# Eight experts on one core: the first weight load goes behind GpSimd's memsets, and ScalarE takes casts from VectorE

## The chip, the core and the metric

The kernel runs on one core of a Trainium2 chip. A core has TensorE (matmul), VectorE, ScalarE, GpSimd and SyncE (SP), each with its own instruction stream, and 16 DMA engines that move data between the chip's memory (DRAM) and the core's on-chip memories SBUF and PSUM. In the profile TensorE is PE with its weight loads as PEld, VectorE is DVE, ScalarE is ACT, GpSimd is POOL. DMAs are issued here by SP (loads and stores without a change of type) and by GpSimd (the weights, which are cast from fp32 to fp16 on the way, and some of the rest). The metric is the device time of one execution in microseconds (us), as the median of several runs; lower is better.

## The reference

Eight experts, each with 256 rows of x (512 wide), a hidden layer of 2048 with bias and ReLU, and an output layer of 512 with bias. All inputs are fp32, and so is the output.

```python
n_experts, capacity, hidden, expert_hidden = 8, 256, 512, 2048
h = np.matmul(x, w1) + b1[:, np.newaxis, :]
h = np.maximum(h, 0)
return (np.matmul(h, w2) + b2[:, np.newaxis, :]).astype(np.float32)
```

Each expert has a w1 of 512 x 2048 and a w2 of 2048 x 512, 4 MB each in fp32, 2 MB (2048 KB) as fp16 in SBUF. All weights together are 64 MB to be read once.

## The kernel before

**Stages.** The kernel goes through the experts with a lag: step s does the first layer of expert s (four matmuls over 512 inputs for each of 16 blocks j of 128 hidden units, line 289, into the four PSUM tiles `ph`) and, from step 3 on, the second layer of expert s - 3 (b2 by a matmul with ones at line 304, then 32 matmuls at line 319 into `po`). ScalarE evicts each `ph` with bias and ReLU to `hT` (line 107) and moves finished `po` to the output tiles (line 119); for the last two experts VectorE evicts half.

**Loads and queues.** GpSimd's queue carries, in this order: w1 of expert 0 and b2 (lines 349 to 353, ahead of everything else on GpSimd), w1 of experts 1 and 2, and then in turn w1 of expert s, w2 of expert s - 3, and at step 4 x of the last four experts. There are three buffers each for w1 and w2, so a load from the fourth on waits until the matmuls have finished with its buffer (`ph_full` and `po_full`). SP's queue carries x of expert 0, x of expert 1, b1, and x of experts 2 and 3 (line 348), and at the end two of the stores.

**The head.** `first_loads` and `first_turns` are ordered by a planner, which places semaphores by the data that each instruction needs. GpSimd sets four small tiles (lines 357 to 360); VectorE turns a block of them (361) and ScalarE copies from it an identity matrix (364). VectorE casts x of experts 0 and 1 to fp16 (366); TensorE turns them with the identity (373) and VectorE copies the result to `xT` (374). VectorE also turns b1 (376). Then comes the section (`tile_critical`, lines 382 to 389), whose semaphores are written out by hand. All engines but GpSimd enter it once all that was issued ahead of it is done, loads included; GpSimd goes in without that wait, issues w1 of experts 1 and 2, and waits for the same things at `wait_critical_data_deps`. In the section ScalarE casts x of experts 2 and 3 (194), and VectorE turns them (223). SP waits for each weight load and raises the counts `w1_in` and `w2_in`, for which TensorE waits.

Of the kernel before, what the change touches and what calls it, by code (L numbers as in the profile page):

```python
# [10 lines left out]
def kernel(  # L11
# [9 lines left out]
    nc = tc.nc  # L21
# [3 lines left out]
    E, T, H = x.shape  # L25
# [3 lines left out]
    nKC = H // P  # L29
# [4 lines left out]
    NW = 3  # L34
# [5 lines left out]
    GROUP_OF = {f + i: (f, n) for f, n in GROUPS.items() for i in range(n)}  # L40
# [11 lines left out]
    w1_sb = w1_f[:, 0 : NW * nKC * M].rearrange("p (n kc m) -> p n kc m", n=NW, kc=nKC)  # L52
    w2_sb = sb("w2sb", [P, NW, nJ, H])
    hT = sb("hTsb", [P, NH, nJ, T])
    xT = sb("xTsb", [P, NX, nKC, T])
    x16 = {f: sb(f"x16_{f}", [P, n * nTB, H]) for f, n in FIRST.items()}
    grouped = {f: sb(f"outg{f}", [P, n * nTB, H], fp32) for f, n in GROUPS.items()}
    pair = [sb(f"pair{i}", [P, nTB, H], fp32) for i in range(2)]
    b2_sb = sb("b2sb", [1, E * H])
# [10 lines left out]
    def sem(name):  # L70
        return nc.alloc_semaphore(name)

    s_x = sem("s_x")
    s_w1 = {e: sem(f"s_w1_{e}") for e in range(1, E)}
    s_w2 = {(e, h): sem(f"s_w2_{e}_{h}") for e in range(E) for h in range(2 if e in CUT else 1)}
    s_out = {e: sem(f"s_out{e}") for e in (0, 4, E - 2)}
    memsets = sem("memsets")
    cast = sem("cast")
    xT_full = sem("xT_full")
    w1_in = sem("w1_in")  # L80
# [5 lines left out]
    po_free_d = sem("po_free_d")  # L86
# [36 lines left out]
    def scalar_from(e):  # L123

        return 0 if e in GROUP_OF else nTB // 2
# [4 lines left out]
    x32 = {e: pair[e] for e in range(2)}  # L130
    x32[2] = grouped[0][:, 0 : FIRST[2] * nTB, :]

    def w1_of(e):
        return w1[e].rearrange("(p kc) m -> p kc m", kc=nKC)

    def x_of(first):
        n = FIRST[first]
        return x[first : first + n].rearrange("e (p r) h -> (e p) r h", r=n * nTB)
# [1 line left out]
    def run_sync():  # L140
        s = nc.sync
        for step in range(E + LAG):
            if step < E:
                if step in s_w1:
                    s.wait_ge(s_w1[step], 16)
                s.sem_inc(w1_in, 1)  # L146
            if step >= LAG:
                e = step - LAG
                for h in range(2):
                    if (e, h) in s_w2:  # L150
                        s.wait_ge(s_w2[e, h], 16)
                    s.sem_inc(w2_in, nQ // 2)  # L152
                    if e == E - 1 and h == 0:
                        s.wait_ge(po_free_a, E)
                        s.wait_ge(po_free_d, E)
                        s.dma_start(out=out_of(E - 2, 1), in_=pair[0]).then_inc(s_out[E - 2], 16)

    def run_gpsimd():
        g = nc.gpsimd

        def load_w1(e):
            if e >= NW:
                g.wait_ge(ph_full, nJ * (e - NW + 1))
            g.dma_start(out=w1_sb[:, e % NW], in_=w1_of(e)).then_inc(s_w1[e], 16)  # L164

        def load_w2(e):
            if e >= NW:
                g.wait_ge(po_full, ENDS * (e - NW + 1))
            src = w2[e].rearrange("(p j) h -> p j h", j=nJ)
            cuts = (0, CUT[e], nJ) if e in CUT else (0, nJ)  # L170
            for h, (lo, hi) in enumerate(zip(cuts, cuts[1:])):
                g.dma_start(  # L172
                    out=w2_sb[:, e % NW, lo:hi], in_=src[:, lo:hi]).then_inc(s_w2[e, h], 16)

        for step in range(1, E + LAG):
            if step < E:
                if step == 4:
                    g.dma_start(out=x16[step], in_=x_of(step)).then_inc(s_x, 16)
                load_w1(step)
            if step == NW - 1:  # L180
                tc.wait_critical_data_deps()
            if step >= LAG:
                load_w2(step - LAG)
        g.wait_ge(s_w2[E - 1, 0], 16)
        for first in sorted(GROUPS, reverse=True):
            done = 1 + first + GROUPS[first]
            g.wait_ge(po_free_a, done)
            g.dma_start(out=out_of(first, GROUPS[first]), in_=grouped[first]).then_inc(  # L188
                s_out[first], 16)
    def run_scalar():  # L190
        a = nc.scalar
        a.sem_inc(ph_free, NPH)
        a.sem_inc(po_free_a, 1)  # L193
        a.copy(out=x16[2], in_=x32[2]).then_inc(cast, 1)  # L194
        for step in range(E + LAG):
            if step < E:
                for j in range(nJ):
                    a.wait_ge(ph_full, nJ * step + j + 1)
                    relu(step, j).then_inc(ph_free, 1)
            if step >= LAG:  # L200
                e = step - LAG
                a.wait_ge(po_full, ENDS * (e + 1))
                for k in range(result(e)[3]):
                    ins = evict(e, scalar_from(e), nTB, k, a.copy)
                ins.then_inc(po_free_a, 1)

    def run_vector():
        v = nc.vector
        v.sem_inc(po_free_d, 1 + len(GROUP_OF))
        v.sem_inc(xT_full, 2)  # L210
        def turn(e):
            first, n, at = X_OF[e]
            R, wide = n * nTB, P // n
            if at == 0:
                v.wait_ge(*((cast, 1) if first == 2 else (s_x, 16)))
            if e >= NX:
                v.wait_ge(ph_full, nJ * (e - NX + 1))
            to = xT[:, e % NX].rearrange("p kc (r i) -> p kc r i", r=R)
            for half in range(wide // B):
                p0 = at * wide + half * B  # L220
                for b in range(nB):
                    src = x16[first][p0 : p0 + B, :, b * (H // nB) : (b + 1) * (H // nB)]
                    ins = v.transpose(  # L223
                        out=to[b * B : (b + 1) * B, :, :, half * B : (half + 1) * B],
                        in_=src.rearrange("p r (i kc) -> p kc r i", kc=nKC))
            ins.then_inc(xT_full, 1)

        turn(2)
        turn(3)
        for e in range(E):  # L230
            if e + NX < E:
                turn(e + NX)
            if scalar_from(e):
                v.wait_ge(po_full, ENDS * (e + 1) - 1)
                for k in range(result(e)[3]):
                    ins = evict(e, 0, scalar_from(e), k, v.tensor_copy)
                ins.then_inc(po_free_d, 1)

    def run_tensor():
        t = nc.tensor  # L240
        mult, mod, least = (getattr(mybir.AluOpType, n) for n in ("mult", "python_mod", "min"))
        xT_f = xT.rearrange("p n kc t -> p (n kc t)")
        w2_f = w2_sb.rearrange("p n j h -> p (n j h)")
# [25 lines left out]
        with t.Fori(0, E + LAG) as s:  # L269
            with t.If(s < E):  # L270
# [8 lines left out]
                with t.Fori(0, nJ // NPH):  # L279
                    w1_j = val(w1_at, (NW - 1) * nKC * M + nJ - NPH)  # L280
                    for i in range(NPH):
                        if i % 2 == 0:
                            t.wait_ge(ph_free, val(due, E * nJ, 1))
                        for kc in range(nKC):
                            if kc % 2 == 0:
                                ahead(w1_cols(w1_j, i, kc), w1_cols(w1_j, i, kc + 1), weights=True)
                            if i % 2 == 1 and kc == nKC - 1:
                                t.reg_add(due, due, 2)
                            ins = t.matmul(  # L289
                                out=ph[i][:, 0:T],  # L290
# [9 lines left out]
            with t.If(s >= LAG):  # L300
                o = val(o_at, nTB * 512)
                b_e = val(b_at, (E - 1) * H)
                for tb in range(nTB):
                    t.matmul(  # L304
                        out=po_f[:, bass.ds(o + tb * 512, H)],
# [6 lines left out]
                with t.Fori(0, nQ):  # L312
# [4 lines left out]
                    for tb in range(nTB):  # L317
                        for j in range(QJ):
                            ins = t.matmul(  # L319
                                out=po_f[:, bass.ds(o + tb * 512, H)],  # L320
# [20 lines left out]
    def first_loads():  # L341
        for to, rows in (
            (x32[0], x_of(0)),
            (x32[1], x_of(1)),
            (b1_rows, b1.rearrange("e (b i) -> (e b) i", b=nB)),
            (x32[2], x_of(2)),
        ):
            tc.keep_in_program_order(nc.sync.dma_start(out=to, in_=rows))  # L348
        for to, rows in (
            (w1_sb[:, 0], w1_of(0)),  # L350
            (b2_sb, b2.rearrange("e h -> (e h)").rearrange("(o f) -> o f", o=1)),
        ):
            tc.keep_in_program_order(nc.gpsimd.dma_start(out=to, in_=rows))

    def first_turns():
        g, v, a, t = nc.gpsimd, nc.vector, nc.scalar, nc.tensor
        g.memset(steps, 0.0)
        g.memset(ident, 0.0)
        g.memset(ones1, 1.0)
        g.memset(steps.rearrange("p n c -> p (n c)")[:, :: B + 1], 1.0)  # L360
        v.transpose(out=steps_turned, in_=steps)  # L361
        for b in range(nB):
            part = slice(b * B, (b + 1) * B)
            a.copy(out=ident[part, part], in_=steps_turned[part, :, 0])  # L364
        for e in range(2):
            v.tensor_copy(out=x16[e], in_=x32[e])  # L366
        for e in range(2):
            pt = ph[2 + e].bitcast(fp16)
            to = pt.rearrange("p (kc r i) -> p kc r i", kc=nKC, r=nTB)
            for r in range(nTB):  # L370
                rows = x16[e][:, r, :].rearrange("p (i kc) -> p kc i", kc=nKC)
                for kc in range(nKC):
                    t.transpose(out=to[:, kc, r, :], in_=rows[:, kc, :], identity=ident)  # L373
            v.tensor_copy(out=xT[:, e], in_=pt.rearrange("p (kc t) -> p kc t", kc=nKC))  # L374
        for b in range(nB):
            v.transpose(  # L376
                out=b1T[b * B : (b + 1) * B, nB - 1 - b : nB - 1 - b + nJ * B],
                in_=b1_rows.rearrange("r (i j) -> r j i", j=nJ))
# [49 lines left out]
```

## Time and profile before

| what | value |
|---|---|
| time, median of 3 runs | 180.91 us (180.85 to 181.17) |
| the profiled execution's own time | 180.94 us |
| its span, first to last instruction | 178.8 us |
| TensorE busy | 131.9 us (74%) |
| ScalarE busy | 82.3 us (46%) |
| VectorE busy | 40.5 us (23%) |
| GpSimd's DMA queue, share of 16 engines | 95.2% |
| moved by DMA, mean rate | 40.98 MB, 229 GB/s |

Times in the trace are counted from the start of the span. A row of the order of time reads: start, duration, engine, line, operation, output<-input, number of instructions, and in brackets the engine's idle time before it and what ended it. POOLq, SPq and so on are the instruction streams where they issue DMAs. In rows by stretch each engine has its busy time and number of instructions; then come TensorE's granted clock, the mean busy share of the DMA engines and the rate. DMA rows count fp16 bytes for the weights, as they are written, while twice as many are read.

### The profile page before, as it was taken

To read this page: it belongs to the slowest core of one execution; us is meant where nothing else is said; L and a number is where in the kernel's file an instruction comes from. 1 tells how busy PE (TensorE), PEld (TensorE's weight loads), DVE (VectorE), ACT (ScalarE), POOL (GpSimd) and SP (SyncE) were. 2 spreads that over 40 slices of the span, in tenths; PEclk is the share of its full clock that TensorE was granted. 3 is DMA by queue.
4 is the path that set the end of the run, shared out by engine and by line. 5 is a ranking of instruction groups with operands and counts; after the bars stand their busy time and mean duration, and the time that the engine had idled before them with its cause. 6 is when DMAs were issued, how large, how long until landed. Compare 5 with 4: busy or idle time off the path is not lost.

```text
span 178.8 us, 2881 instructions
## 1 busy us (share of the span) xinstructions
PE 131.9 (74%) x800; PEld 87.4 (49%) x800; DVE 40.5 (23%) x43; ACT 82.3 (46%) x156; POOL 13.8 (8%) x30
## 2 busy tenths in 40 slices
PE   0002299696969995899959995799599997998940
PEld 0002178575858742785348643674178543443410
DVE  0274399500000299992000000000000000001010
ACT  2002448585867804883098506970488303131010
POOL 7200000302020101001010001000200002001000
PEclk9999999999999999699987999999969999999995
DMA  5999989999999998998998999999899899999995
GB/s 206 278 255 273 236 176 235 235 202 209 236 220 191 235 224 187 235 231 180 235 235 191 220 235 213 198 235 224 187 235 231 180 235 205 205 235 202 323 456 249
DMA packets 3825, 40.98 MB, mean 229 GB/s; under 512 B 448, under 2 KB 464, under 8 KB 1136
## 3 DMA queue, kind: packets, MB, share of 16 engines
q0 software_dynamic: 3056, 37.76, 95.2%
q1 hardware_dynamic: 768, 3.21, 4.6%
q14 instruction: 1, 0.01, 0.0%
HBM read 71.39 MB, written 4.19 MB: 423 GB/s over the span
## 4 chain that ended last, share of the span: by engine, by line
DMA 62%; PE 18%; ACT 6%; DVE 6%; issue 2%; SPq 1%; ACTq 0%; DVEq 0%
DMA w1sb<-in_w_dram 43%; DMA outg<-in_x_dram 10%; PE ph L289 10%; DMA w2sb<-in_w_dram 9%; PE po L319 8%; DVE xTsb L223 6%; ACT hTsb L107 5%; ACT x L194 1%; SPq L348 1%; PE po L304 0%; ACT pair L119 0%; ACTq L423 0%; SPq L146 0%; SPq L152 0%; ACTq L193 0%
## 5 line engine op out<-in xcount | busy, mean ns | idle before, releaser
L289 PE MATMUL ph<-xTsb,w1sb 128*128 x512 | 69.0, 295 | 20.6 <-SPq L146 9.2
L289 PEld LDWEIGHTS ph<-xTsb,w1sb 128*128 x512 | 59.4, 148 | 31.4 <-issue 28.1
L107 ACT ACTIVATE hTsb<-ph,b1T 128x256 f16<-128x256 f32 x128 | 56.9, 475 | 15.4 <-PE ph L289 15.1
L319 PE MATMUL po<-w2sb,hTsb 128*128 x256 | 56.8, 379 | 1.7 <-SPq L152 1.6
L319 PEld LDWEIGHTS po<-w2sb,hTsb 128*128 x256 | 25.0, 98 | 32.3 <-issue 4.8
L119 ACT COPY outg<-po 32x1024 f32<-32x1024 f32 (+1 forms) x20 | 20.1, 1007 | 43.3 <-PE po L319 43.2
L223 DVE STREAM_TRANSPOSE xTsb<-x 32x512 f16<-32x512 f16 (+1 forms) x32 | 31.0, 969 | 31.1 <-DMA x<-in_x_dram 27.7
L119 DVE COPY pair<-po 128x512 f32<-128x512 f32 x2 | 1.4, 692 | 88.0 <-PE po L319 88.0
L373 PE MATMUL ph<-ident,x 128*128 128x128 f16 x16 | 1.9, 308 | 16.8 <-ACT ident L364 16.8
L172 POOL DMA_DIRECT2D w2sb<-in_w_dram x10 | 5.3, 534 | 70.4 <-PE po L319 70.4
L373 PEld LDWEIGHTS <-x 128*128 128x128 f16 x16 | 1.6, 142 | 16.7 <-issue 16.7
L164 POOL DMA_DIRECT2D w1sb<-in_w_dram x7 | 4.2, 599 | 64.4 <-PE ph L289 64.2
L119 ACT COPY pair<-po 128x512 f32<-128x512 f32 x2 | 1.2, 586 | 13.4 <-PE po L319 13.4
L364 ACT COPY ident<-hTsb 32x32 f16<-32x32 f16 x4 | 1.0, 240 | 13.6 <-DVE hTsb L361 13.6
L304 PE MATMUL po<-b2sb,ones 1*128 x16 | 4.8, 378 | 0.9 <-issue 0.8
L376 DVE STREAM_TRANSPOSE b1T<-b1rows 32x512 f32<-32x512 f32 x4 | 4.1, 1022 | 4.1 <-DMA b1rows<-in_b_dram 4.1
L194 ACT CAST x<-outg 128x2048 f16<-128x2048 f32 x1 | 1.9, 1899 | 3.7 <-DMA outg<-in_x_dram 3.7
L304 PEld LDWEIGHTS po<-b2sb,ones 1*128 1x128 f16 x16 | 1.5, 91 | 3.6 <-issue 3.3
L366 DVE CAST x<-pair 128x1024 f16<-128x1024 f32 x2 | 1.4, 694 | 4.7 <-DMA pair<-in_x_dram 4.7
L188 POOL DMA_DIRECT2D out_dram<-outg x2 | 1.1, 538 | 16.1 <-DMA w2sb<-in_w_dram 16.1
L374 DVE COPY xTsb<-ph 128x1024 f16<-128x1024 f16 x2 | 1.4, 692 | 2.4 <-PE ph L373 2.4
L364 ACT ACT_TABLE_LOAD x1 | 1.3, 1283 | 0.7 <-PEq L412 0.7
(12 smaller groups left out, 5.0 us busy)
## 6 DMA issues: line engine op xcount, KB each, us to landing
w1sb<-in_w_dram POOLq DMA_DIRECT2D x8, 2048.0 KB, 30.4
w2sb<-in_w_dram POOLq DMA_DIRECT2D x6, 2048.0 KB, 43.6
w2sb<-in_w_dram POOLq DMA_DIRECT2D x2, 1024.0 KB, 27.8
out_dram<-outg POOLq DMA_DIRECT2D x1, 2048.0 KB, 11.5
w2sb<-in_w_dram POOLq DMA_DIRECT2D x1, 1280.0 KB, 16.8
pair<-in_x_dram SPq DMA_DIRECT2D x2, 512.0 KB, 3.8
outg<-in_x_dram SPq DMA_DIRECT2D x1, 1024.0 KB, 17.8
x<-in_x_dram POOLq DMA_DIRECT2D x1, 1024.0 KB, 27.9
```

Of the source, the lines that this page charges most:

```text
L107: return nc.scalar.activation(out=to, in_=columns, func=relu_of, bias=b1T[:, at : at + 1], scale=1.0)
L119: return copy(out=t.rearrange("p (tb s) h -> p tb s h", s=split)[at : at + rows, lo:hi, k, :], in_=po[k * rows : (k + 1) * rows, e % 2, lo ...
L164: g.dma_start(out=w1_sb[:, e % NW], in_=w1_of(e)).then_inc(s_w1[e], 16)
L172: g.dma_start(out=w2_sb[:, e % NW, lo:hi], in_=src[:, lo:hi]).then_inc(s_w2[e, h], 16)
L194: a.copy(out=x16[2], in_=x32[2]).then_inc(cast, 1)
L223: ins = v.transpose(out=to[b * B : (b + 1) * B, :, :, half * B : (half + 1) * B], in_=src.rearrange("p r (i kc) -> p kc r i", kc=nKC))
L289: ins = t.matmul(out=ph[i][:, 0:T], lhsT=w1_cols(w1_j, i, kc), rhs=x_cols[kc], start=(kc == 0), stop=(kc == nKC - 1),)
L304: t.matmul(out=po_f[:, bass.ds(o + tb * 512, H)], lhsT=ones1, rhs=b2_sb[0:1, bass.ds(b_e, H)], start=True, stop=False, skip_group_check=True,)
L319: ins = t.matmul(out=po_f[:, bass.ds(o + tb * 512, H)], lhsT=hT_f[:, bass.ds(h_e + (j * T + tb * P), P)], rhs=w2_f[:, bass.ds(w_e + j * H, ...
L364: a.copy(out=ident[part, part], in_=steps_turned[part, :, 0])
L373: t.transpose(out=to[:, kc, r, :], in_=rows[:, kc, :], identity=ident)
L376: v.transpose(out=b1T[b * B : (b + 1) * B, nB - 1 - b : nB - 1 - b + nJ * B], in_=b1_rows.rearrange("r (i j) -> r j i", j=nJ))
```

## The change

There are four edits, all at the head of the program.

1. The loads of w1 of expert 0 and of b2 leave `first_loads` and become the first two issues of GpSimd in the section. So they stand behind the four memsets on GpSimd. They get semaphores of their own: SP now waits for the load of expert 0 as for the others, and TensorE waits for b2 as its first act in the section. These two loads are no longer among what the engines wait for when they enter the section.
2. ScalarE instead of VectorE casts x of experts 0 and 1.
3. Of the two copies of turned x from PSUM to `xT`, that of expert 1 goes to ScalarE.
4. Two increments of semaphores at the start of the section go from VectorE to ScalarE.

As the planner orders it, VectorE's head is then: the turn of the small block, two of the four b1 turns, the copy of expert 0's turned x, the other two b1 turns. Before, it was: the two casts, four b1 turns, the turn of the small block, the two copies. ScalarE's head is: four identity copies, the two casts, the copy of expert 1's turned x.

```diff
-    s_w1 = {e: sem(f"s_w1_{e}") for e in range(1, E)}
+    s_w1 = [sem(f"s_w1_{e}") for e in range(E)]
+    s_b2 = sem("s_b2")
...
     def run_sync():
-                if step in s_w1:
-                    s.wait_ge(s_w1[step], 16)
+                s.wait_ge(s_w1[step], 16)
                 s.sem_inc(w1_in, 1)
...
     def run_gpsimd():
+        load_w1(0)
+        g.dma_start(
+            out=b2_sb, in_=b2.rearrange("e h -> (e h)").rearrange("(o f) -> o f", o=1)
+        ).then_inc(s_b2, 16)
         for step in range(1, E + LAG):
...
     def run_scalar():
         a.sem_inc(po_free_a, 1)
+        a.sem_inc(po_free_d, 1 + len(GROUP_OF))
+        a.sem_inc(xT_full, 2)
         a.copy(out=x16[2], in_=x32[2]).then_inc(cast, 1)
...
     def run_vector():
-        v.sem_inc(po_free_d, 1 + len(GROUP_OF))
-        v.sem_inc(xT_full, 2)
...
     def run_tensor():
         t = nc.tensor
+        t.wait_ge(s_b2, 16)
...
     def first_loads():
-        for to, rows in (
-            (w1_sb[:, 0], w1_of(0)),
-            (b2_sb, b2.rearrange("e h -> (e h)").rearrange("(o f) -> o f", o=1)),
-        ):
-            tc.keep_in_program_order(nc.gpsimd.dma_start(out=to, in_=rows))
...
     def first_turns():
         for e in range(2):
-            v.tensor_copy(out=x16[e], in_=x32[e])
+            a.copy(out=x16[e], in_=x32[e])
...
-            v.tensor_copy(out=xT[:, e], in_=pt.rearrange("p (kc t) -> p kc t", kc=nKC))
+            copy = (v.tensor_copy, a.copy)[e]
+            copy(out=xT[:, e], in_=pt.rearrange("p (kc t) -> p kc t", kc=nKC))
```

More of the change, by code (lines that the diff above doesn't have):

```diff
@@ L73 @@
     s_x = sem("s_x")
-    s_w1 = {e: sem(f"s_w1_{e}") for e in range(1, E)}
+    s_w1 = [sem(f"s_w1_{e}") for e in range(E)]
+    s_b2 = sem("s_b2")
     s_w2 = {(e, h): sem(f"s_w2_{e}_{h}") for e in range(E) for h in range(2 if e in CUT else 1)}
     s_out = {e: sem(f"s_out{e}") for e in (0, 4, E - 2)}
-    memsets = sem("memsets")
     cast = sem("cast")
@@ L131 @@
     x32[2] = grouped[0][:, 0 : FIRST[2] * nTB, :]
-    def w1_of(e):
-        return w1[e].rearrange("(p kc) m -> p kc m", kc=nKC)
     def x_of(first):
@@ L163, in load_w1 @@
                 g.wait_ge(ph_full, nJ * (e - NW + 1))
-            g.dma_start(out=w1_sb[:, e % NW], in_=w1_of(e)).then_inc(s_w1[e], 16)
+            g.dma_start(out=w1_sb[:, e % NW], in_=w1[e].rearrange("(p kc) m -> p kc m", kc=nKC)).then_inc(s_w1[e], 16)
         def load_w2(e):
```

## The prediction

> **What bounds the kernel now.** I read the page first, then busy time by stretches, then the chain of waits.
>
> ```profile
> span 178.8 us, 2881 instructions
> PE 131.9 (74%) x800; PEld 87.4 (49%) x800; DVE 40.5 (23%) x43; ACT 82.3 (46%) x156; POOL 13.8 (8%) x30
> DMA  5999989999999998998998999999899899999995
> q0 software_dynamic: 3056, 37.76, 95.2%
> q1 hardware_dynamic: 768, 3.21, 4.6%
> ```
>
> No compute engine is near full: TensorE is busy for 74% of the span, all others for less than half. The row of the DMA engines stands at 8 or 9 tenths in 38 of its 40 slices, and GpSimd's queue (q0, all the weights) holds 95.2% of the engines' time. The stretches say it without the rounding of slices; the last two columns are the DMA share and GB/s, and a packet is counted where it begins, so that a share can pass 1.
>
> ```profile
> core 0: us, PE busy (x) PEld busy (x) DVE busy (x) ACT busy (x) POOL busy (x), PEclk, DMA share, GB/s
> 0.00:2.50 2.50, 0.00 (x0) 0.00 (x0) 0.00 (x0) 1.28 (x1) 1.45 (x7) 1.00 0.21 49
> 2.50:4.75 2.25, 0.00 (x0) 0.00 (x0) 0.59 (x1) 0.00 (x0) 2.09 (x5) 1.00 1.02 410
> 20.00:40.00 20.00, 15.87 (x112) 13.58 (x112) 11.24 (x16) 13.99 (x28) 1.59 (x3) 1.00 0.98 210
> 40.00:80.00 40.00, 33.19 (x232) 25.55 (x232) 18.30 (x15) 26.01 (x54) 3.18 (x6) 0.96 1.02 216
> 80.00:120.00 40.00, 33.66 (x210) 22.43 (x208) 1.48 (x2) 23.43 (x44) 1.59 (x3) 0.96 1.02 216
> 120.00:164.00 44.00, 40.08 (x202) 21.14 (x202) 0.69 (x1) 16.01 (x26) 2.12 (x4) 0.96 1.02 216
> 172.00:176.00 4.00, 0.00 (x0) 0.00 (x0) 0.00 (x0) 0.51 (x1) 0.00 (x0) 0.78 0.95 406
> 2.50:177.50 175.00, 131.91 (x800) 87.42 (x800) 40.51 (x43) 81.02 (x155) 12.39 (x24) 0.96 1.02 233
> ```
>
> From 2.5 to 177.5 us, 175 of the 178.8 us, the 16 DMA engines are full (share 1.02), in each long stretch as in the sum. The weights go at a steady 216 GB/s, so one weight load of 2048 KB (2.1 MB as it is written) occupies them for 2.1 / 0.216 = 9.7 us. The chain of waits shows the same from the other side:
>
> ```profile
> 2.12 17.83 DMA outg<-in_x_dram
> 42.44 28.68 DMA w1sb<-in_w_dram
> 81.71 47.53 DMA w1sb<-in_w_dram
> 147.57 16.84 DMA w2sb<-in_w_dram
> 164.60 3.62 PE po L319 x16
> 168.26 3.64 PE po L319 x16
> 171.92 0.59 ACT pair L119
> ```
>
> A w1 load that needs 9.7 us lands 28.68 and 47.53 us after its issue: the rest is standing in the queue behind earlier loads. The end is set by the last w2 load (its first part lands at 147.57 + 16.84 = 164.41), then 7.3 us of matmul, an eviction and the stores. So the span is the start of the DMA stream, plus its total work, plus idle time of its engines, plus this tail. An edit counts only as far as it changes one of these four.
>
> **The change part by part.** *The first w1 load behind the memsets.* The head of GpSimd's program and of SP's:
>
> ```profile
> 0.74 0.86 SPq L348 DMA_DIRECT2D pair<-in_x_dram  x2
> 1.25 0.67 POOL L353 DMA_DIRECT2D w1sb<-in_w_dram  x1 [0.80 <-POOLq L412]
> 2.41 0.98 POOL L357 MEMSET hTsb<- 128x1024 f16 x1
> 3.98 1.53 POOL L164 DMA_DIRECT2D w1sb<-in_w_dram  x2 [0.16 <-issue]
> ```
>
> From the first of four memsets to the first issue in the section are 3.98 - 2.41 = 1.57 us, entry to the section included. In the changed kernel the memsets start where the w1 load of expert 0 does now (1.25), and that load is issued at 1.25 + 1.57 = 2.82. The b2 load and the w1 loads of experts 1 and 2 follow in the same order, so the queue's order is unchanged, and every later issue of GpSimd waits for matmuls as before. What does the delay of 1.57 us do to the engines?
>
> ```profile
> 4.50:4.75 0.25, 0.00 (x0) 0.00 (x0) 0.25 (x1) 0.00 (x0) 0.25 (x1) 1.00 0.96 393
> 4.75:5.00 0.25, 0.00 (x0) 0.00 (x0) 0.10 (x1) 0.00 (x0) 0.25 (x2) 1.00 4.68 1000
> 5.00:6.00 1.00, 0.00 (x0) 0.00 (x0) 0.62 (x1) 0.00 (x0) 0.51 (x1) 1.00 0.09 20
> ```
>
> And SP's loads of the head, by size and time from issue to landing (us):
>
> ```profile
> pair<-in_x_dram SPq DMA_DIRECT2D x2, 512.0 KB, 3.8
> outg<-in_x_dram SPq DMA_DIRECT2D x1, 1024.0 KB, 17.8
> b1rows<-in_b_dram SPq DMA_DIRECT2D x1, 64.0 KB, 8.5
> ```
>
> The jump to 1000 GB/s at 4.75 to 5.00 is the beginning of the long weight packets: share 4.68 of 0.25 us is 1.17 us of work laid on every engine at once, which runs through the nearly empty row behind it. So the w1 load's data begins some 3.6 us after its issue (4.85 - 1.25). Until then the x loads of SP's queue alone fill the engines, at 410 GB/s. That queue holds 2 x 512 + 1024 + 64 KB, 2.16 MB; the two halves for experts 0 and 1 (1.05 MB) are through at about 4.9, and the rest, b1 and x of experts 2 and 3 (1.11 MB), would last 1.11 / 0.41 = 2.7 us more, to 7.6. These are the loads that now take 8.5 and 17.8 us to land, because they share the engines with w1. If the w1 load's data begins 3.6 us after the new issue, at 6.4, the engines still have 1.2 us of x to carry: no idle time, and what was done first is only done second. Cost: nothing. The cover is the x of experts 2 and 3; without it the cost would be 6.4 - 4.9 = 1.5 us. The unknown is the 3.6 us. Its lower end doesn't matter (any start before 7.6 costs nothing). For its upper end I take the slowest neighbour:
>
> ```profile
> L164 POOL DMA_DIRECT2D w1sb<-in_w_dram x7: 530/530/999, 4.0 to 81.7; - x7
> ```
>
> and what ran beside that one:
>
> ```profile
> 4.16 0.69 DVE L366 CAST x<-pair 128x1024 f16<-128x1024 f32 x1 [4.16 <-DMA pair<-in_x_dram]
> ```
>
> An issue at line 164 takes 530 ns, one of the seven 999, the one at the section's start, beside VectorE's cast. Even with 0.47 us for that and as much as a whole transpose of VectorE (1.25 us, quoted below) in the way, the data would begin at 8.1, and the idle time would be 0.5 us. I take 6.4, since it is the same instruction with the same queue before it.
>
> The Trainium skill, page "SBUF — State Buffer", section "SBUF: two separate sides", says that a VectorE copy or cast in its two-port mode locks GpSimd out of writing the descriptors of its DMAs, so that such a DMA starts late. The 999 ns beside the cast agree with it, though one case shows no cause. By that page the change, which takes both casts from VectorE, would let the w1 load's data begin sooner after its issue than 3.6 us, and the rival below of idle engines would fall away; the sum would stay at nothing, because an earlier start finds the engines full of x.
>
> *Casts, eviction and VectorE's order.* VectorE's list becomes the turn of the identity's steps, two b1 turns, one xT copy, two b1 turns; ScalarE gets both casts and the other xT copy. What the pieces take and when they end now:
>
> ```profile
> 10.19 4.13 DVE L376 STREAM_TRANSPOSE b1T<-b1rows 32x512 f32<-32x512 f32 x4 [4.11 <-DMA b1rows<-in_b_dram]
> 14.35 1.25 DVE L361 STREAM_TRANSPOSE hTsb<-hTsb 128x1024 f16<-128x1024 f16 x1
> 15.62 1.00 ACT L364 COPY ident<-hTsb 32x32 f16<-32x32 f16 x4 [13.60 <-DVE hTsb L361]
> 16.77 1.87 PE L373 MATMUL ph<-ident,x 128*128 128x128 f16 x16 [16.77 <-ACT ident L364]
> 22.09 10.15 PE L289 MATMUL ph<-xTsb,w1sb 128*128 x64 [3.46 <-issue]
> ```
>
> ```profile
> L194 ACT CAST x<-outg 128x2048 f16<-128x2048 f32 x1 | 1.9, 1899 | 3.7 <-DMA outg<-in_x_dram 3.7
> ```
>
> Today the steps' turn stands behind the b1 turns, which wait for b1 until 10.19. In the changed kernel the memsets end near 2.7, the turn (1.25) near 3.9, the identity's copies (1.00) near 4.9, ScalarE's two casts (half of 1.9 us each, by the cast of twice the width) near 6.8, the PE turns (1.87) near 8.7, the copies out near 10. VectorE's four b1 turns (4.13), once b1 has landed near 7, end near 12. All engines then wait at the section's entry for x of experts 2 and 3; it shares the engines with w1 from 6.4 on and lands at 13 to 17. The first w1 matmul can't start before w1 itself: 7.6 us of stream plus 9.7 is 17.3, plus b2 behind it and the waits, about 18.5. So this part has 5 us of cover, and brings the first matmuls from 22.09 to about 18.5. That is not on the path: the w1 load of expert 3 would be issued about 4 us earlier, into a queue that still holds the loads of experts 1 and 2 (to 7.6 + 3 x 9.7 = 36.7). What is late next is the stream itself. Cost and gain: nothing.
>
> *New waits.* SP waits for the first w1 load before it raises its count, and TensorE waits for b2 once. Behind them stand stage 0's matmuls and nothing else; b2 is 8 KB next in the queue. With 4 us in hand, nothing.
>
> **Sum.** 0 for the w1 load, 0 for the casts and the order, 0 for the waits; I add 0.1 us as an estimate for fewer switches between the two queues, since the share stands at 1.02 where both overlap a little. The profiled execution took 180.94 us (span 178.8 and 2.1 around it), 0.03 over the median of 180.91. Forecast 181.0.
>
> **Rivals.**
> *The engines run dry at the head (slower).* The x of experts 2 and 3 isn't ready behind the first two, and the engines stand idle from 4.9 until the w1 load's data begins. For it: today b1 and that x land 8.5 and 17.8 us after their issue, and no row shows them alone. Against: both were issued by about 2.1, and the engines never had a gap in which to show it. Place: 4.9 to 7.6 us; it decides from the moment at which the w1 data begins with nothing else queued. Full price 6.4 - 4.9 = 1.5, which gives 182.4; with only a late start after the x, up to 0.5, 181.4.
> *The chain is right as it is drawn (faster).* The chain runs through x of experts 2 and 3, its cast, its turns and the first two stages of matmuls; if the issues made earlier by this really pulled the stream, all would move by 22.09 - 18.5, 3.6 us, to 177.3. For it: the order of the chain. Against: no stretch has spare engines to take the earlier issues. A smaller gain would need the same spare time.
> *The compute becomes late (slower).* If ScalarE's longer list or the wait for b2 kept stage 0 back so long that the w1 load of expert 3 came after 36.7, the queue would run dry. With a start at 18.5 and 10.15 us for the stage it is issued near 29; 8 us would have to be lost. Each us beyond that costs one: with 10 us lost, 183.
>
> **How the numbers follow.** Forecast 0.64, with its own range 180.6 to 181.3; engines dry at the head 0.20; the chain right or any spare time found 0.12; late compute 0.04. About 0.2% (0.36 us) is what a measurement of this kernel can tell from no change. The two slower rivals make 0.24, the faster one 0.12, the forecast 0.64. The range runs from 180.5 up to the full price of dry engines, 182.4; what it leaves out is most of the faster rival and the late compute.
>
> **What would show it.** Right: the share of 2.5 to 177.5 us stays at 1.02, with no empty stretch between 5 and 8 us that no long packets cover; the GpSimd row of the first w1 load stands near 2.8, the x of experts 2 and 3 lands well before 17.8 us after its issue, the first w1 matmul is near 18.5, and the last w2 load's landing stays within 0.3 us of 164.41. Wrong: a stretch near 5 to 6.5 us at a share far below 1 with no packets begun before it, or the last w2 landing moved by more than 0.3 us.

## The result and the profile after

The changed kernel takes 181.64 us (median of 13 runs, 180.85 to 181.95) against 180.96 us of the kernel before (13 runs, 180.85 to 181.25): a ratio of 1.0031, 95% interval 1.0019 to 1.0043. It is slower by 0.6 (the ratio) to 0.7 us (the medians). The forecast was 181.0, no change. 181.64 lies in the range that was given, 180.5 to 182.4, but above the forecast's own range of 180.6 to 181.3, which had most of the chance. The profiled execution took 181.65 us.

The page after, the parts that were shown of before:

```profile
span 179.9 us, 2874 instructions
PE 132.7 (74%) x800; PEld 87.7 (49%) x800; DVE 38.5 (21%) x40; ACT 85.5 (48%) x159; POOL 13.4 (7%) x30
q0 software_dynamic: 3056, 37.76, 94.7%
q1 hardware_dynamic: 768, 3.21, 4.9%
```

The same bytes on the same queues. The weights' queue holds 94.7% of a longer span, and SP's queue (q1) holds 4.9% instead of 4.6% for the same 3.21 MB. The stretches after:

```profile
core 0: us, PE busy (x) PEld busy (x) DVE busy (x) ACT busy (x) POOL busy (x), PEclk, DMA share, GB/s
2.50:4.75 2.25, 0.00 (x0) 0.00 (x0) 0.92 (x1) 1.24 (x5) 2.12 (x4) 1.00 1.02 400
4.75:5.75 1.00, 0.18 (x2) 0.18 (x3) 0.00 (x0) 0.77 (x1) 0.00 (x0) 1.00 1.02 193
1.50:25.00 23.50, 6.22 (x36) 4.78 (x37) 9.83 (x12) 8.37 (x13) 2.90 (x8) 1.00 1.00 249
20.00:40.00 20.00, 16.99 (x120) 14.55 (x121) 11.25 (x16) 14.02 (x30) 1.59 (x3) 1.00 1.02 218
40.00:80.00 40.00, 31.34 (x215) 23.86 (x214) 17.22 (x14) 24.06 (x50) 3.18 (x6) 0.91 1.02 217
80.00:120.00 40.00, 33.78 (x210) 22.53 (x209) 2.56 (x3) 23.38 (x43) 1.59 (x3) 0.96 1.02 217
```

From 20 us on the rates are those of before (216). In the first 25 us, before and after:

```profile
1.50:25.00 23.50, 4.78 (x30) 3.94 (x31) 10.79 (x13) 4.42 (x9) 3.85 (x8) 1.00 1.03 260
```

260 GB/s before, 249 after. All x loads of SP's queue are through by 25 us in both, so what is missing, 11 GB/s x 23.5 us = 0.26 MB, is weights, and at 0.216 MB per us that is 1.2 us of stream. (This is coarse: a packet is counted where it begins, and 0.26 MB is just one packet of 16 KB on each of the 16 engines.) Most of it goes missing right behind the x of experts 0 and 1: SP's loads move at 400 GB/s up to 4.75 us, and at 193 GB/s in the us behind it. A row of 193 GB/s at a share of 1.02 could also be weights, which go at 216, but no packet of the weights' queue q0 begins in it:

```profile
q1 hardware_dynamic: 75, 0.19, 102.0%
```

So SP's own packets take longer there. The trace's single packets say how much: the first seven pieces of 8 KB of the x of experts 2 and 3 take 1.0 to 1.3 us each, and most of the later ones 0.31 to 0.32, as from the first one on in the kernel before. The second weight load, by the mean end of its last 16 packets, is 0.85 us late, and stays so to the end. That is about the sum of what the first 25 us lose: 0.2 us more of idle time per engine, and 0.7 us more of SP packets that take longer than is usual for their size. A load has landed with its last packet, and that comes 0.9 to 1.1 us late. The whole lag is there again at the end, in the chain of waits:

```profile
148.81 16.69 DMA w2sb<-in_w_dram
165.69 3.62 PE po L320 x16
169.36 3.64 PE po L320 x16
173.02 0.59 ACT pair L119
```

The first part of the last w2 load lands at 148.81 + 16.69 = 165.50, 1.09 us later than before (164.41); behind it the tail is as before. The head of the two issuing programs:

```profile
0.74 0.95 POOL L353 MEMSET hTsb<- 128x1024 f16 x1 [0.29 <-POOLq L409]
0.74 0.86 SPq L349 DMA_DIRECT2D pair<-in_x_dram  x2
2.12 0.42 SPq L349 DMA_DIRECT2D outg<-in_x_dram  x1
2.36 0.67 POOL L160 DMA_DIRECT2D w1sb<-in_w_dram  x1 [0.22 <-issue]
```

The w1 load of expert 0 is issued at 2.36 (2.82 was forecast: the memsets start at 0.74, half a us sooner than the load did), 1.1 us later than before. When does its data begin? The rows of a quarter us rise when its packets of 16 KB join:

```profile
5.50:5.75 0.25, 0.18 (x2) 0.18 (x3) 0.00 (x0) 0.01 (x1) 0.00 (x0) 1.00 0.92 254
5.75:6.00 0.25, 0.25 (x5) 0.25 (x4) 0.00 (x0) 0.11 (x1) 0.00 (x0) 1.00 0.99 270
6.00:6.25 0.25, 0.25 (x5) 0.25 (x4) 0.00 (x0) 0.25 (x1) 0.00 (x0) 1.00 1.69 393
6.25:6.50 0.25, 0.25 (x4) 0.09 (x1) 0.13 (x1) 0.25 (x1) 0.00 (x0) 1.00 2.08 492
```

It joins at about 6: 13 of its first 16 packets begin from 5.75 to 6.5, the other three after 7, where before 15 of them began at 4.75 to 5.00. The first w1 matmul starts at 20.87 (22.09 before), and that is worth nothing: the loads end later all the same.

### The profile page after: what moved, and what is told of

Same layout as the page of the kernel before. It is cut to its first block, busy times and chain, and to the rows that moved or that the text cites. A ratio compares the mean times of both kernels' runs of the same rounds, so it can differ in the third digit from the quotient of the medians.

```text
span 179.9 us, 2874 instructions
## 1 busy us (share of the span) xinstructions
PE 132.7 (74%) x800; PEld 87.7 (49%) x800; DVE 38.5 (21%) x40; ACT 85.5 (48%) x159; POOL 13.4 (7%) x30
## 3 DMA queue, kind: packets, MB, share of 16 engines
q0 software_dynamic: 3056, 37.76, 94.7%
q1 hardware_dynamic: 768, 3.21, 4.9%
## 4 chain that ended last, share of the span: by engine, by line
DMA 46%; PE 25%; ACT 15%; DVE 6%; issue 4%; SPq 1%; ACTq 0%
DMA w1sb<-in_w_dram 28%; PE ph L290 12%; PE po L320 12%; ACT hTsb L107 11%; DMA w2sb<-in_w_dram 9%; DMA outg<-in_x_dram 9%; DVE xTsb L223 6%; ACT outg L119 2%; ACT x L196 1%; SPq L349 1%; PE po L305 1%; ACT pair L119 0%; ACTq L420 0%; SPq L148 0%; SPq L142 0%
## 5 line engine op out<-in xcount | busy, mean ns | idle before, releaser
L119 ACT COPY outg<-po 32x1024 f32<-32x1024 f32 (+1 forms) x20 | 20.1, 1006 | 43.1 <-PE po L320 42.9
L362 ACT CAST x<-pair 128x1024 f16<-128x1024 f32 x2 | 2.1, 1044 | 0.4 <-DMA pair<-in_x_dram 0.4
L357 DVE STREAM_TRANSPOSE hTsb<-hTsb 128x1024 f16<-128x1024 f16 x1 | 1.2, 1245 | 2.2 <-POOL hTsb L356 2.2
## 6 DMA issues: line engine op xcount, KB each, us to landing
outg<-in_x_dram SPq DMA_DIRECT2D x1, 1024.0 KB, 16.6
```

The source lines that it names most:

```text
L119: return copy(out=t.rearrange("p (tb s) h -> p tb s h", s=split)[at : at + rows, lo:hi, k, :], in_=po[k * rows : (k + 1) * rows, e % 2, lo ...
```

## Experiments

Times are medians, with the ratio to runs of the kernel before on the same chip and its 95% interval; each has 4 to 13 runs.

| run | time, us | ratio to before | interval |
|---|---|---|---|
| changed kernel | 181.64 | 1.0031 | 1.0019 to 1.0043 |
| casts alone | 181.04 | 1.0008 | 0.9996 to 1.0020 |
| w1 and b2 into the section alone | 181.97 | 1.0056 | 1.0040 to 1.0072 |
| changed, memsets on VectorE | 180.77 | 0.9997 | 0.9981 to 1.0014 |
| changed, one more memset | 181.74 | 1.0040 | 1.0027 to 1.0053 |
| changed, three more memsets | 182.04 | 1.0055 | 1.0040 to 1.0069 |
| changed, b1 last | 181.89 | 1.0031 | 1.0006 to 1.0055 |
| changed, x of 2, 3 on ScalarE's queue | 183.09 | 1.0103 | 1.0082 to 1.0123 |
| changed, b1 first | 182.04 | 1.0042 | 1.0020 to 1.0063 |
| before, compute made late | 181.41 | 1.0022 | 0.9999 to 1.0045 |
| changed, x of 2, 3 by GpSimd | 181.26 | 1.0014 | 0.9998 to 1.0030 |
| both remedies | 180.73 | 0.9982 | 0.9964 to 0.9999 |
| changed, x of 2, 3 in two loads | 184.47 | 1.0192 | 1.0166 to 1.0217 |

**Which part of the change costs?** The kernel before with the casts and the second copy on ScalarE:

```diff
-            v.tensor_copy(out=x16[e], in_=x32[e])
+            a.copy(out=x16[e], in_=x32[e])
...
-            v.tensor_copy(out=xT[:, e], in_=pt...)
+            copy = (v.tensor_copy, a.copy)[e]
+            copy(out=xT[:, e], in_=pt...)
```

> The kernel before with only the casts and the second copy moved to ScalarE; the loads of w1 of expert 0 and b2 stay ahead of the memsets. Theory (the late first w1 load leaves the DMA engines partly idle at 4.75 to 6 us): no change, 180.8 to 181.2 us, and the first long packets begin at 4.75 to 5.0 us as before. Rival (ScalarE's casts disturb the x loads that they run beside): 181.4 to 181.8, with x packets that take longer from 4 us on.

181.04, no difference from before. And the changed kernel with these edits undone, so that only the move of the loads is left:

> The changed kernel with the casts and copies back on VectorE; w1 of expert 0 and b2 are issued in the section behind the memsets. Theory of the late load: as slow as the changed kernel, 181.4 to 181.9, with the first long packets near 5.9 us and a share below 1 between 4.75 and 5.75 us. Rival of ScalarE's casts: 180.8 to 181.2.

181.97, just above the theory's range: the whole loss is in this part, if anything a little more of it than in the changed kernel. Then the memsets out of the load's way:

```diff
-        g.memset(steps, 0.0)
+        v.memset(steps, 0.0)
...
```

(and so for the other three.)

> The changed kernel with the four memsets on VectorE, so that GpSimd enters the section at once and issues w1 of expert 0 near 0.9 us, its data beginning near 4.4 us. Theory of the late load: the whole loss comes back, 180.6 to 181.1, since the long packets begin before x of experts 0 and 1 is through. Rival (the loss comes from the load being in the section, or from the new waits, wherever it stands): 181.4 to 181.9.

180.77, as before. The loads may stand in the section and have their waits; that isn't what costs. These three settle the place: it is the first w1 load behind the memsets.

**Does the loss grow with the delay?** One more memset on GpSimd, into a tile that nothing reads, ahead of the section:

```diff
+    idle = sb("idle", [P, 1024])
...
         g.memset(steps.rearrange("p n c -> p (n c)")[:, :: B + 1], 1.0)
+        g.memset(idle, 0.0)
```

> The changed kernel with one more memset of 128x1024 (about 1 us) behind the four, so that w1 of expert 0 is issued near 3.3 us and its data begins near 6.8 us. Theory that SP's loads fill the engines alone only in part: another 0.3 to 1 us, 181.9 to 182.7. Rival, my prediction's cover (x of experts 2 and 3 fills the engines until 7.6 us, and the loss is a single hiccup at its beginning): no more than 0.2 us over the changed kernel, 181.4 to 181.9.

181.74, in the rival's range: 0.6 us more delay cost 0.1 us, which the two intervals don't tell from nothing. With three of them, the load issued at 4.94:

> The changed kernel with three more memsets of 128x1024 on GpSimd (about 1 us each) behind the four, so that w1 of expert 0 is issued near 5 us and GpSimd issues nothing between 2 and 5 us. Theories A and B (SP's queue starves the engines): the share of 4.75 to 5.75 us is as low as in the run with one more memset (about 0.7), and x of experts 2 and 3 shows its whole course alone; the time grows by another 0.5 to 1.5 us, to 182.3 to 183.3. Rival C (GpSimd's issues at 2.4 to 5.2 us disturb SP's queue): the share stays near 1 from 4.75 us to the end of the x loads near 7.6 us, and only what is idle after that is lost, 181.9 to 182.5.

182.04, below the range of theories A and B: 2.6 us more delay than in the changed kernel cost about 0.4 us. So the loss is not one us for each us of delay; most of it comes with the first. Here is SP's queue alone with the engines, one and three more memsets (columns as in the stretches above), before the w1 load's data begins:

```profile
2.50:4.75 2.25, 0.00 (x0) 0.00 (x0) 0.92 (x1) 1.24 (x5) 2.25 (x5) 1.00 1.02 392
4.75:5.75 1.00, 0.17 (x2) 0.18 (x3) 0.00 (x0) 0.77 (x1) 0.46 (x1) 1.00 0.69 223
5.75:6.75 1.00, 0.87 (x8) 0.60 (x6) 0.77 (x1) 0.96 (x1) 0.00 (x0) 1.00 0.70 287
```

```profile
2.50:4.75 2.25, 0.00 (x0) 0.00 (x0) 0.91 (x1) 1.24 (x5) 2.13 (x3) 1.00 1.01 390
4.75:5.75 1.00, 0.18 (x2) 0.19 (x3) 0.00 (x0) 0.93 (x2) 1.00 (x3) 1.00 1.35 279
5.75:6.75 1.00, 0.92 (x9) 0.66 (x8) 0.97 (x1) 0.89 (x1) 1.00 (x3) 1.00 0.71 287
```

The x of experts 0 and 1 runs at 390 GB/s; behind it, with nothing else on the engines, the x of experts 2 and 3 gets 223 to 287 for two us. It is slow in two ways. In the first run the engines are only 0.7 full in both rows. In the second 1.35 and 0.71 make a mean of 1.03: the engines are busy, but with packets that take long (several of the first pieces of 8 KB 1.3 to 1.5 us). There GpSimd issues its first weight load at 4.94, just as this load begins, so this run alone can't rule out that GpSimd's issues disturb it (rival C, in whose range the time came out). The next run does: in it GpSimd issues its loads when it does in the changed kernel, and the x load starts fast.

**What in SP's queue is slow?** b1 behind the large x load, so that this one stands right behind x of expert 1:

```diff
             (x32[1], x_of(1)),
-            (b1_rows, b1.rearrange("e (b i) -> (e b) i", b=nB)),
             (x32[2], x_of(2)),
+            (b1_rows, b1.rearrange("e (b i) -> (e b) i", b=nB)),
```

> The changed kernel with SP's last two loads exchanged: x of experts 2 and 3 ahead of b1. Theory A (the small b1 load in the middle, two packets of 2 KB on each engine, empties the queue, and the load behind it starts slowly): the share stays at 1 until the long packets begin, and the time comes back to 180.8 to 181.2 us. Theory B (the third and later loads of SP's queue are slow to start whatever they are): still partly idle from 4.75 us on, 181.4 to 181.9.

The time is 181.89, outside of A's range, and its runs spread from 180.73 to 182.99. But the head did what A expected:

```profile
4.75:5.75 1.00, 0.18 (x2) 0.19 (x3) 0.00 (x0) 1.00 (x2) 0.00 (x0) 1.00 1.05 377
1.50:25.00 23.50, 1.99 (x16) 1.55 (x16) 6.03 (x6) 5.32 (x9) 2.89 (x8) 1.00 1.03 258
```

Right behind x of expert 1 the large load starts at 377 GB/s, not 193, and of the loss in 1.5 to 25 us only 2 x 23.5 / 216 = 0.2 us is left; the second weight load is 0.25 us late by the mean of its last packets, not 0.85. The time doesn't follow (its ratio is that of the changed kernel), since another cost has come in: b1 lands late and the matmuls start late, which is taken up below. To part the two, b1 first of all:

> The changed kernel with b1 as the first of SP's loads, so that x of experts 2 and 3 stands right behind x of expert 1, and b1 is early (in the run with b1 last it landed at 19 us, and the first w1 matmul moved to 25.8). Theory A (the small b1 load between the x loads empties the queue): most of the loss goes, 180.9 to 181.3 us, and the matmuls start near 21 us. Theory B (the start of any further load is exposed while SP's queue is alone): no better than the changed kernel, 181.4 to 181.9.

182.04, again outside of A's range, with the matmuls in time (21.55):

```profile
1.50:3.00 1.50, 0.00 (x0) 0.00 (x0) 0.83 (x1) 0.52 (x1) 1.28 (x5) 1.00 0.61 153
4.75:5.75 1.00, 0.00 (x0) 0.00 (x0) 0.99 (x2) 0.85 (x1) 0.00 (x0) 1.00 0.91 336
1.50:25.00 23.50, 5.54 (x33) 4.30 (x34) 9.07 (x11) 7.91 (x12) 2.90 (x8) 1.00 1.00 252
```

The large load again doesn't start slowly (336). This time the first stretch is slow: behind b1 stands x of expert 0, and 1.5 to 3 us has 153 GB/s where the changed kernel has 216. The rate of 1.5 to 25 us is 252, so 8 x 23.5 / 216 = 0.9 us is lost there (0.65 by the mean of the last packets of the second weight load). GpSimd's last store is issued 1.6 us later than before. The rest of that is unevenness: two of the last 16 packets of each weight load end 0.6 to 0.9 us behind the others, and a load has landed only with its last.

Then the load from ScalarE's queue:

```diff
-            (x32[2], x_of(2)),
...
+        tc.keep_in_program_order(nc.scalar.dma_start(out=x32[2], in_=x_of(2)))
```

> The changed kernel with x of experts 2 and 3 loaded from ScalarE's queue instead of SP's, so that it can start beside x of expert 0. Theory that SP's queue is what starves the engines (A and B alike): both queues together fill the engines until 7.5 us, share 1 throughout, 180.8 to 181.2 us. Rival C (the 16 engines cannot be filled by these loads alone between 4.75 and 6 us, whichever queue they come from, for example since GpSimd's issues run beside them): 181.4 to 181.9.

183.09, outside of both ranges: now x of experts 2 and 3 lands in 7.3 us and those of 0 and 1 in 11.4 instead of 4.0, and the matmuls start at 26.36. Its head has 414 GB/s in 4.75 to 5.75 us, and 158 in 1.5 to 3, this without b1 ahead; so the slow first stretch of the run with b1 first doesn't show by itself that b1 made it. At last the size of the pieces, with b1 where the changed kernel has it:

```diff
-            (x32[2], x_of(2)),
+            (x32[2][:, 0:2], x_of(2)[:, 0:2]),
+            (x32[2][:, 2:4], x_of(2)[:, 2:4]),
```

> The changed kernel with SP's load of x of experts 2 and 3 cut in two, so that its packets are 4 KB as those of experts 0 and 1 instead of 8 KB. If the long packets are what starts slowly: the share stays full at 4.75 to 6 us and the time comes back to 180.9 to 181.3. Rival (any load that SP's queue starts there alone is slow, or the w1 data waits for what SP has queued): 181.4 to 182.

184.47, beyond either range (the profiled execution, the fastest of the six, took 183.12), with the matmuls at 26.96. The slow start is there with pieces of half the size:

```profile
4.75:5.75 1.00, 0.18 (x2) 0.18 (x3) 0.00 (x0) 0.76 (x1) 0.00 (x0) 1.00 1.03 125
```

So the head rates put the slow start on the load that stands right behind the small b1 load on SP's queue: it is there with b1 ahead of the large load (193, 223, 279 and, in halves, 125 GB/s) and gone with b1 elsewhere (377, 336). It isn't the size of its pieces. In the times this could not be seen, since each of these edits brought a cost of its own, and why a load behind a small one starts slowly isn't settled. It needn't be special to small loads: the first eight packets of x of expert 0, with nothing before them, take 0.2 to 0.8 us in the changed kernel where 0.16 is usual.

**Take that load away.** The changed kernel with GpSimd loading x of experts 2 and 3 behind b2, w1 as late as it was:

```diff
         ).then_inc(s_b2, 16)
+        g.dma_start(out=x16[2], in_=x_of(2)).then_inc(cast, 16)
...
-        a.copy(out=x16[2], in_=x32[2]).then_inc(cast, 1)
```

(SP's load of it goes, the wait counts 16, and the increment of `xT_full` goes back to VectorE.)

> The changed kernel with x of experts 2 and 3 loaded by GpSimd behind b2, cast on the way, instead of by SP: the cover over the late w1 load is taken away, and ScalarE's cast of it goes. My prediction's price of the missing cover: the engines stand idle from about 4.95 us to the first long packets at 5.9 us, 0.9 to 1 us of loss in all, 181.8 to 182.1. Rival (what costs is only the slow start of that x load, which now begins behind long packets): 180.9 to 181.4.

181.26, which its interval doesn't tell from before, and my price for a missing cover (181.8 to 182.1) is refuted. The trace shows why:

```profile
2.36 0.67 POOL L160 DMA_DIRECT2D w1sb<-in_w_dram  x1 [0.22 <-issue]
```

```profile
4.75:5.00 0.25, 0.00 (x0) 0.00 (x0) 0.00 (x0) 0.25 (x1) 0.25 (x1) 1.00 3.33 844
5.00:5.25 0.25, 0.00 (x0) 0.00 (x0) 0.00 (x0) 0.25 (x1) 0.15 (x1) 1.00 2.35 500
1.50:25.00 23.50, 9.44 (x64) 7.71 (x64) 12.73 (x16) 9.46 (x19) 3.43 (x9) 1.00 1.04 237
```

The w1 load is issued at 2.36 as in the changed kernel, and its data begins at 4.75 to 5.25, as in the kernel before, where it is issued 1.1 us earlier. The simplest reading is that the load waits until the x of experts 0 and 1 is through, and where SP has more queued, for some of that too. (The delay without a queue shows in the runs with late matmuls, below: w1 of expert 3 is issued there when the loads before it are nearly or quite through, at 35.65, 36.28 and 36.76, and its first data follows 1.2 us later in each. The rate of 237 is no loss: the x of 1024 KB counts as 512 KB here, cast on the way, which is 22 GB/s of this stretch; 237 + 22 = 259.) The late issue alone costs nothing that this run can tell: the second weight load is 0.08 us late.

Both remedies in one kernel, memsets on VectorE and this load:

> The changed kernel with both remedies that worked alone: the four memsets on VectorE (w1 of expert 0 is issued near 1.3 us) and x of experts 2 and 3 loaded by GpSimd behind b2. If the slow start of that x load is the whole loss and the issue of w1 costs nothing by itself, this is as the runs with either remedy, 180.7 to 181.2 us, and no faster than the kernel before by more than 0.2%, since the stream of loads is the bound. Rival (the earlier matmuls, which start near 17.5 us, still bring something): 180.0 to 180.5.

180.73, 0.9982 of before with an interval that ends at 0.9999: faster than the changed kernel, and than the kernel before by a margin at the edge of what was measured. Its matmuls start at 17.32, 4.8 us earlier than before, and the last w2 lands no earlier:

```profile
164.74 1.06 POOL L189 DMA_DIRECT2D out_dram<-outg  x2 [16.18 <-DMA w2sb<-in_w_dram]
```

against 164.69 for that issue in the kernel before. The stream is the bound, and early compute brings no more than that margin.

**Late compute does cost.** Three of the runs above have their first w1 matmul at 25.83, 26.36 and 26.96, and took 181.89, 183.09 and 184.47 (for the first the ratio alone shows no cost beyond the changed kernel's). Who TensorE waited for in its first layer (us in total, times, longest), first with b1 last:

```profile
PE ph L290 <- issue: 25.5, 8, 18.3
PE ph L290 <- ACT hTsb L107: 10.6, 4, 2.7
```

and in the changed kernel:

```profile
PE ph L290 <- SPq L142: 10.6, 4, 4.6
PE ph L290 <- ACT hTsb L107: 1.9, 2, 1.4
```

With late compute it waits for ScalarE's evictions instead of for the loads that SP announces, and an expert takes 20.1 to 20.2 us (the groups of matmuls with b1 last, by their start):

```profile
65.56 7.08 PE L320 MATMUL po<-w2sb,hTsb 128*128 x32
85.65 7.08 PE L320 MATMUL po<-w2sb,hTsb 128*128 x32
105.88 7.08 PE L320 MATMUL po<-w2sb,hTsb 128*128 x32
```

Two weight loads take 2 x 9.7 = 19.4 us, so matmuls that start too late don't catch up, and fall further behind. At the end the chain runs in all three over matmuls back to back and waits for no load, with b1 last:

```profile
161.64 7.01 PE po L320 x32
168.65 0.53 PE po L305 x2
169.19 7.03 PE po L320 x32
```

The stream itself loses time too, once. In these runs the w1 load of expert 3, which waits for stage 0's matmuls, is issued at 35.65 to 36.76 instead of 31.48, when the first three w1 loads are nearly or quite through. Here are the changed kernel, b1 last, x on ScalarE's queue and x in two loads:

```profile
35.00:40.00 5.00, 4.84 (x40) 4.38 (x41) 0.00 (x0) 4.20 (x10) 0.00 (x0) 1.00 1.03 220
35.00:40.00 5.00, 3.15 (x28) 2.69 (x26) 2.54 (x4) 2.78 (x7) 1.60 (x3) 1.00 0.92 167
35.00:40.00 5.00, 3.13 (x27) 2.67 (x27) 3.06 (x5) 3.03 (x8) 1.59 (x3) 1.00 0.88 157
35.00:40.00 5.00, 3.27 (x30) 2.97 (x28) 3.68 (x6) 2.89 (x7) 1.59 (x3) 1.00 0.90 161
```

Most of the first packets of this load also take 1.7 to 2.3 us instead of 1.23. Together the stream falls back by another 0.9, 1.4 and 1.2 us.

What slack there was shows in the kernel before, in the same view (us in total, times, longest):

```profile
PE ph L289 <- SPq L146: 9.2, 4, 2.5
```

TensorE waits for a late w1 load four times, 9.2 / 4 = 2.3 us each. An attempt to make the compute late in the kernel before:

```diff
+        for to in spare:
+            a.copy(out=to, in_=x32[2])
         a.sem_inc(ph_free, NPH)
```

> The kernel before with two more casts of x of experts 2 and 3 on ScalarE (1.9 us each, into tiles that nothing reads) ahead of its first increment of ph_free, so that the first w1 matmul moves from 22.1 to about 25.9 us; the loads are untouched. Theory of a near second bound (as in the run with b1 last, where a stage took 20.3 us against 19.4 us of loads and TensorE never caught up): 1 to 2 us slower, 182 to 183. Rival, my prediction's figure for late compute (8 us have to be lost first): no change, 180.8 to 181.2.

181.41, outside both ranges, interval 0.9999 to 1.0045: inconclusive. The increment didn't wait for the copies, so the first matmul kept its time (22.24) and only the evictions were late; the second stage starts at 35.99 instead of 34.00. The w1 load of expert 3 is issued at 34.52, and the stream doesn't thin out (210 GB/s in 35 to 40 us, as before). What two us of late compute cost, if anything, isn't shown.

## Why the prediction was right or wrong

**The bound** was read rightly. The weights' stream sets the time; a lag of about 1 us made in the first 25 us stood unchanged 140 us later, and a gain of 4.8 us in the start of the matmuls brought at most 0.2%. With that the rival that took the chain of waits at its word is refuted.

**The failed step** is the cost of the late w1 load: "no idle time, and what was done first is only done second. Cost: nothing." It cost 0.7 us in the medians and moved the last w2 landing of the profiled execution by 1.1, well over the 0.3 us that the prediction named as a sign of being wrong. That the time lies in the stated range is luck as far as the forecast's mechanism goes: the upper end came from the price of a rival. Two things in the step were wrong.

First, the cover. I let the x of experts 2 and 3 fill the engines at the 410 GB/s that the x of experts 0 and 1 reaches. No row of the trace showed that load alone behind b1; where it is, it gets 193 to 287 GB/s for its first one or two us. The 410 would have been near right with b1 elsewhere (377, 336). In the kernel before it begins behind w1 packets, and the rate of the first 25 us shows no such loss. The work was conserved, but the rate at which it is done was not. The rival of engines that run dry named the place (4.9 to 7.6 us) and the sign; its full 1.5 us did not come. Its condition, that the x of experts 2 and 3 isn't ready behind the first two, is close to what the runs show.

Second, the 3.6 us from issue to first data. I took it for a delay that moves with the issue. In the run without SP's large load it is 2.4 to 2.9 us, and the data begins when it did in the kernel before; on engines that were nearly or quite free it is 1.2 us. So what I had measured was, by the simplest reading, mostly waiting for the x of experts 0 and 1. That the changed kernel again shows about 3.6 us (issued at 2.36, data at about 6) is chance: there it waited for part of the next x load as well. So my 1.5 us for a missing cover was wrong in kind: without the cover nothing was lost.

**Casts, order and waits** at nothing: right, by the run with the casts alone. Their times were less well forecast: the identity's turn, the casts and the PE turns came as worked out within 1 us, but x of experts 2 and 3 landed at 2.12 + 16.6 = 18.7 us, not 13 to 17, and the section and the first matmul followed it (20.87, not 18.5). The 0.1 us that I added for fewer switches between the queues shows in no run.

The Trainium skill, page "SBUF — State Buffer", section "SBUF: two separate sides", holds a VectorE copy in its two-port mode to lock GpSimd out of writing DMA descriptors. The run with the casts alone agrees: the longest issue at line 164 falls from 999 to 559 ns when the casts leave VectorE.

```profile
L164 POOL DMA_DIRECT2D w1sb<-in_w_dram x7: 530/530/559, 4.0 to 81.6; - x7
```

But the time doesn't follow it, and the w1 data of the changed kernel did not begin sooner, as I had thought by that page.

**Late compute** was priced too low. "8 us would have to be lost" was counted from a start at 18.5, so up to 26.5, and for the queue that wasn't far off: with starts at 25.83 to 26.96 it ran short, a little sooner than forecast, since the 1.2 us from issue to data were left out. What I had missed is the second limit, TensorE's own: once it waits for evictions instead of loads, an expert takes 20.2 us against 19.4. The three runs, 3.7 to 4.9 us behind the start of before, were 0.6 to 3.5 us slower than it by their ratios, the head's loss included; that the 2.3 us of waiting for each late w1 load are all the slack there is, is argued from these rows and not shown by a run of its own. The compute was not late in the profiled execution of the changed kernel. Whether late compute plays a part in its other executions, whose times spread over 1.1 us where those of before spread over 0.4, was not seen.

## What to carry to other kernels

Work conservation is not enough to call a moved load free: ask at what rate the work that takes its place runs when it is alone, and if no row shows it alone, let that rate be the range. A time from issue to first data was a plain delay here only where the engines were nearly or quite free (1.2 us); with other loads queued it was a place in a line (2.4 to 3.6 us), and moving the issue need not move the data. And the slack of the engine that isn't the bound has two limits: what is still in the queue, and what the engine waits per stage.

## What the runs showed that was not expected

Issued at 1.25 us, the w1 load's data begins near 4.75. Issued at 2.36, it still begins near 4.75 where SP's large x load is taken away, and at about 6 where that load is queued. The load right behind the small b1 load starts slowly on engines that have nothing else to do: 125 to 279 GB/s in the us behind 4.75, against 336 and 377 with b1 elsewhere. Moving b1 cured that and not the time (181.89, 182.04): at the end of the queue it came too late for the compute, and at its head the first stretch had 153 GB/s.
